# Down projection by seven products: product 2 moved ahead of product 7, and two groups of bank-emptying sums given priority on VectorE

## The chip, the cores and the metric

The kernel runs on one core of a Trainium2 chip. The metric is the time of one execution on the device in microseconds (us). Engines are named as in the profile: PE is TensorE (PEld its weight loads), DVE is VectorE, ACT is ScalarE, POOL is GpSimd, SP is SyncE, which issues most DMAs (SPq and POOLq are the queues).

## The reference

One layer of a hybrid trunk on 1024 tokens of width 1024. The change touches only the last part, the feed-forward block:

```
h2 = rms_norm(x, pre_ffn_g[l])
f = (jax.nn.silu(h2 @ w_gate[l]) * (h2 @ w_up[l])) @ w_down[l]
x = x + rms_norm(f, post_ffn_g[l])
```

The hidden width is 2816. All values are float32. The last product, with `w_down`, is called the down phase here, and the last line, a normalisation over the 1024 columns of each token and a sum, is written row by row behind it.

## The kernel before, in words

**Seven products in place of eight.** The down phase treats its two operands as 2 x 2 quadrants (two halves of 512 tokens; two halves of 512 output columns; the hidden width in 11 pairs of 128-row blocks, p = 0 to 10) and forms seven products of sums of quadrants in place of eight plain ones. Each product q is 11 steps (q, p), so there are 77 steps. The list `PQ` sets the order of the products, here 1, 5, 6, 3, 7, 2, 4. The sums of the activations were written to DRAM earlier (`fd`, `fs`) and are read back (L1106); `w_down` is read by L1112; the differences of weights for products 7 and 4 are made on VectorE by L1135.

**Exact operands by splitting.** Each operand of a step is split into a rounded part, made by ScalarE (L78, CAST), and a remainder, made by VectorE (L79). A step then has three matmuls (L1151 rounded x rounded, L1152 rounded x weight remainder, L1153 activation remainder x rounded) for each of four token strips t of 128 tokens: 12 matmuls of 512 columns.

**Blocks.** Steps are prepared in blocks, numbered 0 to 19: 18 blocks of four steps, one of one step, one of four. A block's split operands lie in a buffer `ob`, of which there are two. So the splits of block k+1 can begin when the matmuls of block k-1 are over, that is, when those of block k begin; a full block is 48 matmuls. Raw operands come through a ring of eight tiles of 256 KB, so the loads for a block's steps are issued as the splits of the block before free them. The steps of the last block run strip by strip (all four steps of t = 0, then t = 1, ...), those of all other blocks step by step.

**Banks.** Products accumulate in eight PSUM banks, one per strip: X[t] for products 1, 6, 7 and 4, which run on in the same bank, and Z[t] for 5 and 3, which run on, and for 2, which starts anew. When a product is complete, `after(q, t)` takes out strip t: products 1, 5 and 6 are copied by ScalarE (`kept`); product 3 is added to what was kept of 6 (L1191), 7 to 5 (L1196), 2 to 1 (L1201), all on VectorE; product 4 is read from the bank as it is. Products 3 and 2 give the two column halves of the first token half, 7 and 4 those of the second.

**Rows.** With both column halves of a strip at hand, the chain for its rows is: square and sum on ScalarE (L1164), gain product on GpSimd (L1167), row factor on GpSimd (L1176, L109, L111), two scalings with the sum of x on VectorE (L1182), two writes of 256 KB (L1183). The x of a strip is read from DRAM scratch (`x1d`, L1173). For the first token half this chain hangs on product 2, for the second on product 4.

**What sets the order.** The order of each engine's queue is set at build time by a scheduler that goes by program order and priority; `tc.high_priority()` moves what stands in it ahead. The splits and loads of a block stand in it. At run time each engine takes its queue strictly in that order, and so a waiting instruction holds up all behind it. The changed lines:

Of the kernel before, what the change touches and what calls it, by code (L numbers as in the profile page):

```python
# [11 lines left out]
ALU = mybir.AluOpType  # L12
# [29 lines left out]
def tile_hymba_trunk(ctx, tc, x, w_in, vecs, w_l, w2, a2, g2, w_o, w_gate, w_up, w_down,  # L42
                     gains, consts, out):
    nc = tc.nc
    te, ve, sc, gp, sy = nc.tensor, nc.vector, nc.scalar, nc.gpsimd, nc.sync
# [24 lines left out]
    def wt(name, tag, shape, dtype=F32):  # L70
        return mp.tile(shape, dtype, name=name, tag=tag, bufs=RING[tag])
# [905 lines left out]
    class Gemm:  # L977
# [55 lines left out]
        def after(self, q):  # L1033
            if q == 1:
                self.c11 = wt("c11", "bv", [128, H])
                sc.copy(self.c11, self.X)
            elif q == 2:
                ve.tensor_tensor(out=self.c11, in0=self.Y, in1=self.c11, op=ALU.add)
                self.finish(self.c11, self.c11, 0, 0)
            elif q == 6:  # L1040
                self.c12 = wt("c12", "ez", [128, H])
                sc.copy(self.c12, self.X)  # L1042
            elif q == 7:
                self.c22 = wt("c22", "am", [128, H])
                sc.copy(self.c22, self.X)
                ve.tensor_tensor(out=self.c22, in0=self.Z, in1=self.c22, op=ALU.add)
                self.finish(self.c22, self.c22, 1, 1)
            elif q == 4:
                self.finish(self.X, wt("c21", "e", [128, H]), 1, 0)
            elif q == 3:  # L1050
                ve.tensor_tensor(out=self.c12, in0=self.Z, in1=self.c12, op=ALU.add)
                self.finish(self.c12, self.c12, 0, 1)
# [22 lines left out]
    NP = NHID // 2  # L1075
# [21 lines left out]

    load_gain(1, "KB")
    XT = ["AK"] * 2 + ["Lo"] * 2 + ["Atok"] * 2
    PQ = [1, 5, 6, 3, 7, 2, 4]  # L1100
    steps = [(q, p) for q in PQ for p in range(NP)]
    tres = {}

# [34 lines left out]
    def down_block(block):  # L1138
        ob = tp.tile([128, 4, 2, 2, H], F32R, name="ob", tag="T")
        with tc.high_priority():  # L1140
            for n, (q, p) in enumerate(block):
                split(f_raw(q, p), ob[:, n, 0, 0], ob[:, n, 0, 1])
                split(d_operand(q, p), ob[:, n, 1, 0], ob[:, n, 1, 1])
        return ob

    def down_mm(q, p, ob, n, t):
        f, w = ob[:, n, 0], ob[:, n, 1]
        ts = slice(t * 128, (t + 1) * 128)
        ps = (Z if q in (5, 3, 2) else X)[t]
        st, en = q in (1, 5, 2) and p == 0, p == NP - 1  # L1150
        te.matmul(ps, lhsT=f[:, 0, ts], rhs=w[:, 0], start=st, stop=False, skip_group_check=True)  # L1151
        te.matmul(ps, lhsT=f[:, 0, ts], rhs=w[:, 1], start=False, stop=False, skip_group_check=True)  # L1152
        te.matmul(ps, lhsT=f[:, 1, ts], rhs=w[:, 0], start=False, stop=en, skip_group_check=True)  # L1153

    X, Z = [], []
# [4 lines left out]
    def square(i, dh, src):  # L1160
        if i not in ssq:
            ssq[i] = sp.tile([128, 2], F32, name="ssf", tag=f"ssf{i}", bufs=1)
        junk = wt("junk", "Vtok", [128, H])
        sc.activation(junk, src, AF.Square, accum_out=ssq[i][:, dh:dh + 1])  # L1164

    def scaled(a, dh, eng):
        eng.tensor_tensor(out=a, in0=a, in1=gain[1][:, dh * H:(dh + 1) * H], op=ALU.mult)  # L1167

    def row_scale(i):
        xts = []  # L1170
        for dh in range(2):
            xt = wt("xt", XT[(2 * i + dh) % len(XT)], [128, H])
            sy.dma_start(out=xt, in_=x1d[i * 128:(i + 1) * 128, dh * H:(dh + 1) * H])  # L1173
            xts.append(xt)
        ss = sp.tile([128, 1], F32, name="ss1", tag="ss1")
        gp.tensor_tensor(out=ss, in0=ssq[i][:, 0:1], in1=ssq[i][:, 1:2], op=ALU.add)  # L1176
        return xts, rsqrt_rows(sp, ss, D, "fo", gp)

    def row_out(i, cs, xts, rs):
        for dh in range(2):  # L1180
            a = cs[dh]
            ve.scalar_tensor_tensor(out=a, in0=a, scalar=rs, in1=xts[dh], op0=ALU.mult, op1=ALU.add)  # L1182
            sy.dma_start(out=out[i * 128:(i + 1) * 128, dh * H:(dh + 1) * H], in_=a)  # L1183

    def after(q, t):
        if q in KEPT:
            k = kept[q, t] = wt("kept", KEPT[q][t], [128, H])
            sc.copy(k, (Z if q == 5 else X)[t])
        elif q == 3:
            c = kept[6, t]  # L1190
            ve.tensor_tensor(out=c, in0=Z[t], in1=c, op=ALU.add)  # L1191
            square(t, 1, c)
            scaled(c, 1, gp)
        elif q == 7:
            c = kept[5, t]
            ve.tensor_tensor(out=c, in0=X[t], in1=c, op=ALU.add)  # L1196
            square(4 + t, 1, c)
            scaled(c, 1, gp)
        elif q == 2:
            c = kept[1, t]  # L1200
            ve.tensor_tensor(out=c, in0=Z[t], in1=c, op=ALU.add)  # L1201
            square(t, 0, c)
            scaled(c, 0, gp)
            row_out(t, (c, kept[6, t]), *row_scale(t))
        else:
            square(4 + t, 0, X[t])
            a = wt("c21", "bv", [128, H])
            ve.tensor_tensor(out=a, in0=X[t], in1=gain[1][:, 0:H], op=ALU.mult)
            row_out(4 + t, (a, kept[5, t]), *row_scale(4 + t))
# [3 lines left out]
    for bn, size in enumerate(sizes):  # L1213
        block = steps[s0:s0 + size]
        s0 += size
        ob = down_block(block)
        if bn == len(sizes) - 1:
            for t in range(4):
                for n, (q, p) in enumerate(block):
                    down_mm(q, p, ob, n, t)  # L1220
                after(q, t)
            continue
        for n, (q, p) in enumerate(block):
            if p == 0 and q == 1:
                X += [pB.tile([128, H], F32, name="pdx", tag="b") for t in range(4)]
            elif p == 0 and q == 5:
                Z += [pA.tile([128, H], F32, name="pdz", tag="a") for t in range(2)]
                Z += [pS.tile([128, H], F32, name="pdz", tag=f"c{t}") for t in range(2)]
            for t in range(4):
                down_mm(q, p, ob, n, t)  # L1230
            if p == NP - 1:
                for t in range(4):
                    after(q, t)


# [64 lines left out]
```

## Time and profile before

| | |
|---|---|
| median of three runs | 1303.29 us (1300.52 to 1306.16) |
| the profiled execution | 1306.03 us |
| its span, first to last instruction | 1304.3 us |
| TensorE busy | 1244.5 us, 95% |
| VectorE busy | 941.3 us, 72% |
| ScalarE, GpSimd busy | 540.5 us (41%), 328.5 us (25%) |
| mean granted clock of TensorE | 0.983 |

The span is the time between the first and the last instruction of the profiled execution; its own time is 1.7 us longer. A busy share is an average over all phases. The down phase is the last fifth of the span, from about 1075 us on. A granted clock of 1.00 is 2.4 GHz and 0.50 is 1.2 GHz.

### The profile page before, as it was taken

Reading aid. Unit: us, or ns where it says so; the run is one execution under the profiler, and the core shown is the slowest. Engines: PE = TensorE matmul, PEld = TensorE weight load, DVE = VectorE, ACT = ScalarE, POOL = GpSimd, SP = SyncE. Lnnn points to the kernel's source line nnn. Section 1 sums busy time; section 2 is a strip of 40 time slices with the busy share of each in tenths; the row PEclk is TensorE's granted clock in tenths of the full one; section 3 lists DMA queues with packets and bytes.
Section 4 is the critical chain, followed back from the end, with each engine's and each line's share of the span. In section 5 each row is a group of like instructions: output and inputs, shape, how many; then the busy total and the mean of one; then the engine's idle time right before and its main releaser. Section 6 shows DMA issues by size and latency. Waiting matters only on the chain.

```text
span 1304.3 us, 21097 instructions
## 1 busy us (share of the span) xinstructions
PE 1244.5 (95%) x7924; PEld 1005.8 (77%) x7924; DVE 941.3 (72%) x1784; ACT 540.5 (41%) x1029; POOL 328.5 (25%) x370
## 2 busy tenths in 40 slices
PE   6999999999999999999889999999999999999996
PEld 5878767787777778677677888888888878888884
DVE  5999797988899895563796665565665666666766
ACT  7327436445433332534353333333333353454532
POOL 2121314322232211022543234233323310000212
PEclk9999899999999999999999999999999999999999
DMA  7116332322222112652312322233323248765656
GB/s 243 33 43 207 98 130 98 105 82 87 80 94 68 42 34 74 202 170 98 137 65 98 112 82 102 100 114 113 105 81 114 90 165 276 255 195 172 210 187 210
DMA packets 76119, 162.13 MB, mean 124 GB/s; under 512 B 8880, under 2 KB 9264, under 8 KB 74608
## 3 DMA queue, kind: packets, MB, share of 16 engines
q1 hardware_dynamic: 66128, 126.96, 30.2%
q0 software_dynamic: 6432, 27.53, 5.5%
q10 hardware_dynamic: 3456, 6.29, 1.3%
q8 instruction: 62, 1.02, 0.3%
q14 instruction: 41, 0.34, 0.1%
HBM read 115.39 MB, written 45.35 MB: 123 GB/s over the span
## 4 chain that ended last, share of the span: by engine, by line
PE 45%; DVE 2%; POOL 1%; DMA 1%; issue 1%; ACT 1%; DVEq 0%; SPq 0%; ACTq 0%; POOLq 0%
PE px L1028 6%; PE px L1029 6%; PE px L1030 6%; PE pz L1028 3%; PE pz L1029 3%; PE pz L1030 3%; PE pdx L1152 2%; PE pdx L1153 2%; PE pdx L1151 2%; PE pdz L1152 2%; PE pdz L1151 2%; PE pdz L1153 2%; PE py L1030 1%; PE py L1029 1%; PE py L1028 1%
## 5 line engine op out<-in xcount | busy, mean ns | idle before, releaser
L78 ACT CAST whi<-wraw 128x512 fp32r<-128x512 f32 x111 | 68.6, 620 | 138.1 <-PE px L1029 57.9
L79 DVE TENSOR_TENSOR wlo<-wraw,whi 128x512 fp32r<-128x512 f32 x111 | 78.4, 708 | 53.8 <-ACT whi L78 53.2
L79 DVE TENSOR_TENSOR ob<-wraw,ob 128x512 fp32r<-128x512 f32 x132 | 86.2, 706 | 27.7 <-ACT ob L78 27.6
L78 ACT CAST whi<-wsum 128x512 fp32r<-128x512 f32 x88 | 54.5, 619 | 122.7 <-PE py L1029 36.1
L78 ACT CAST ob<-wraw 128x512 fp32r<-128x512 f32 x132 | 73.2, 618 | 75.1 <-PE pdx L1153 35.0
L79 DVE TENSOR_TENSOR wlo<-wsum,whi 128x512 fp32r<-128x512 f32 x88 | 68.7, 780 | 45.1 <-ACT whi L78 44.6
L250 DVE SCALAR_TENSOR_TENSOR cfa<-cfu,vec,cfa 128x512 f32<-128x512 f32 x120 | 92.3, 799 | 0.8
L103 PE MATMUL prkv<-hT,whi 128*128 128x512 f32 x192 | 82.7, 431 | 5.0 <-DVE lz L369 2.5
L580 DVE TENSOR_TENSOR tm<-TT,Mg 128x2 f32<-128x2 f32 (+30 forms) x248 | 77.7, 313 | 6.0
L993 POOL TENSOR_TENSOR wsum<-wraw 128x512 f32<-128x512 f32 x44 | 59.5, 1353 | 85.7 <-DVE wlo L79 37.7
L105 PE MATMUL prkv<-hT,wlo 128*128 128x512 f32 x192 | 78.1, 407 | 0.0
L104 PE MATMUL prkv<-hT,whi 128*128 128x512 f32 x192 | 78.0, 406 | 0.0
L1152 PE MATMUL pdx<-ob 128*128 128x512 f32 x176 | 69.3, 394 | 4.6 <-DVE ob L79 4.6
L1028 PE MATMUL px<-h2T,whi 128*128 128x512 f32 x176 | 69.8, 397 | 2.1 <-ACT c L1042 1.7
L1029 PE MATMUL px<-h2T,whi 128*128 128x512 f32 x176 | 69.5, 395 | 0.0
L1030 PE MATMUL px<-h2T,wlo 128*128 128x512 f32 x176 | 69.4, 394 | 0.0
L1151 PE MATMUL pdx<-ob 128*128 128x512 f32 x176 | 68.9, 393 | 0.0
L1153 PE MATMUL pdx<-ob 128*128 128x512 f32 x176 | 68.8, 392 | 0.0
L582 DVE TENSOR_REDUCE TT<-tm 128x1 f32<-128x2 f32 (+30 forms) x248 | 63.0, 254 | 6.0
L1167 POOL TENSOR_TENSOR kept<-kept,gain 128x512 f32<-128x512 f32 x12 | 16.7, 1410 | 169.1 <-ACT junk L1164 169.1
L1151 PE MATMUL pdz<-ob 128*128 128x512 f32 x132 | 51.3, 389 | 0.0
L1152 PE MATMUL pdz<-ob 128*128 128x512 f32 x132 | 51.3, 389 | 0.0
(360 smaller groups left out, 3458.7 us busy)
## 6 DMA issues: line engine op xcount, KB each, us to landing
wraw<-in_w_down SPq DMA_DIRECT2D x88, 256.0 KB, 4.0
wraw<-in_w_in SPq DMA_DIRECT2D x44, 256.0 KB, 2.9
wraw<-in_w_gate SPq DMA_DIRECT2D x44, 256.0 KB, 2.7
wraw<-in_w_up SPq DMA_DIRECT2D x44, 256.0 KB, 2.9
fs<-fs POOLq DMA_DIRECT2D x11, 1024.0 KB, 4.6
wraw<-fs SPq DMA_DIRECT2D x44, 256.0 KB, 3.9
fd<-c POOLq DMA_DIRECT2D x33, 256.0 KB, 2.4
wraw<-fd SPq DMA_DIRECT2D x33, 256.0 KB, 4.1
```

What stands on the lines that cost most here:

```text
L78: sc.copy(hi, raw)
L79: ve.tensor_tensor(out=lo, in0=raw, in1=hi.bitcast(F32), op=ALU.subtract)
L103: te.matmul(ps, lhsT=lhi, rhs=rhi, start=start, stop=False)
L104: te.matmul(ps, lhsT=lhi, rhs=rlo, start=False, stop=False)
L105: te.matmul(ps, lhsT=llo, rhs=rhi, start=False, stop=stop)
L250: ve.scalar_tensor_tensor(out=acc, in0=u[:, q:q + H], scalar=v1(V_CFW + i * 31 + q), in1=acc, op0=ALU.mult, op1=ALU.add)
L1028: te.matmul(ps, lhsT=hi[:, k, :], rhs=rhi, start=first and k == 0, stop=False, skip_group_check=True)
L1029: te.matmul(ps, lhsT=hi[:, k, :], rhs=rlo, start=False, stop=False, skip_group_check=True)
L1030: te.matmul(ps, lhsT=lo[:, k, :], rhs=rhi, start=False, stop=k == 3, skip_group_check=True)
L1151: te.matmul(ps, lhsT=f[:, 0, ts], rhs=w[:, 0], start=st, stop=False, skip_group_check=True)
L1152: te.matmul(ps, lhsT=f[:, 0, ts], rhs=w[:, 1], start=False, stop=False, skip_group_check=True)
L1153: te.matmul(ps, lhsT=f[:, 1, ts], rhs=w[:, 0], start=False, stop=en, skip_group_check=True)
```

## The change

Products 7 and 2 change places in `PQ`, so that product 2 comes fifth, 7 sixth and 4 last. The sums of product 3 (now L1192) and product 7 (now L1198) get high priority. The call of `after` moves from behind all four strips of a product's last step into the loop over strips. The arithmetic is the same.

```diff
-    PQ = [1, 5, 6, 3, 7, 2, 4]
+    PQ = [1, 5, 6, 3, 2, 7, 4]
...
         elif q == 3:
             c = kept[6, t]
-            ve.tensor_tensor(out=c, in0=Z[t], in1=c, op=ALU.add)
+            with tc.high_priority():
+                ve.tensor_tensor(out=c, in0=Z[t], in1=c, op=ALU.add)
...
         elif q == 7:
             c = kept[5, t]
-            ve.tensor_tensor(out=c, in0=X[t], in1=c, op=ALU.add)
+            with tc.high_priority():
+                ve.tensor_tensor(out=c, in0=X[t], in1=c, op=ALU.add)
...
             for t in range(4):
                 down_mm(q, p, ob, n, t)
-            if p == NP - 1:
-                for t in range(4):
+                if p == NP - 1:
                     after(q, t)
```

In the changed order, products that follow each other directly meet in the same banks in two places: 3 and 2 in Z (the border of blocks 10 and 11), 7 and 4 in X (inside block 16, whose first two steps are product 7's last and whose other two are product 4's first). Product 2 ends with the third step of block 13.

**VectorE's queue behind product 2.** Before, from the eighth remainder of block 17 on (L1201 is the sum of product 2, `ob` the split operands, `tres` a kept sum of weights):

```order
L79 TENSOR_TENSOR ob<-wraw,ob 128x512
L1201 TENSOR_TENSOR kept<-pdz,kept 128x512
L1135 TENSOR_TENSOR wraw<-wraw,tres 128x512
L1201 TENSOR_TENSOR kept<-pdz,kept 128x512
L1135 TENSOR_TENSOR wraw<-wraw,tres 128x512
L1182 SCALAR_TENSOR_TENSOR kept<-kept,for,xt 128x512 x2
L1135 TENSOR_TENSOR wraw<-wraw,tres 128x512
L1182 SCALAR_TENSOR_TENSOR kept<-kept,for,xt 128x512 x2
L79 TENSOR_TENSOR ob<-wraw,ob 128x512 x2
L1201 TENSOR_TENSOR kept<-pdz,kept 128x512 x2
```

Behind these rows come the other four L1182 with one L1135 among them, and then the eight remainders of block 19. After the change, from the seven first remainders of block 15 on (L1203 is the sum of product 2 now; the first two strips' sums and scalings stand in the same way ahead of these rows, behind block 14's remainders):

```order
L79 TENSOR_TENSOR ob<-wraw,ob 128x512 x7
L1135 TENSOR_TENSOR wraw<-tres,wraw 128x512
L79 TENSOR_TENSOR ob<-wraw,ob 128x512
L1203 TENSOR_TENSOR kept<-pdz,kept 128x512
L1135 TENSOR_TENSOR wraw<-tres,wraw 128x512
L1203 TENSOR_TENSOR kept<-pdz,kept 128x512
L1135 TENSOR_TENSOR wraw<-wraw,tres 128x512
L1182 SCALAR_TENSOR_TENSOR kept<-kept,for,xt 128x512 x2
L1135 TENSOR_TENSOR wraw<-wraw,tres 128x512
L1182 SCALAR_TENSOR_TENSOR kept<-kept,for,xt 128x512 x2
```

The two sets moved from the remainders of blocks 17 to 19 to those of blocks 14 to 16: the first now stands between blocks 14 and 15, the second between 15 and 16.

**VectorE's queue around the sums of product 7.** Before (L1196), between the remainders of block 14 and those of block 15:

```order
L1135 TENSOR_TENSOR wraw<-tres,wraw 128x512 x2
L79 TENSOR_TENSOR ob<-wraw,ob 128x512 x16
L1196 TENSOR_TENSOR kept<-pdx,kept 128x512 x4
L79 TENSOR_TENSOR ob<-wraw,ob 128x512 x8
L1135 TENSOR_TENSOR wraw<-wraw,tres 128x512 x2
```

After the change (L1198), from the first seven remainders of block 16, directly behind the rows shown above, to the eight of block 19:

```order
L79 TENSOR_TENSOR ob<-wraw,ob 128x512 x7
L1135 TENSOR_TENSOR wraw<-wraw,tres 128x512
L79 TENSOR_TENSOR ob<-wraw,ob 128x512
L1135 TENSOR_TENSOR wraw<-wraw,tres 128x512 x3
L79 TENSOR_TENSOR ob<-wraw,ob 128x512 x5
L1198 TENSOR_TENSOR kept<-pdx,kept 128x512 x4
L1135 TENSOR_TENSOR wraw<-wraw,tres 128x512 x2
L79 TENSOR_TENSOR ob<-wraw,ob 128x512 x3
L1135 TENSOR_TENSOR wraw<-wraw,tres 128x512
L79 TENSOR_TENSOR ob<-wraw,ob 128x512 x2
L1135 TENSOR_TENSOR wraw<-wraw,tres 128x512 x2
L79 TENSOR_TENSOR ob<-wraw,ob 128x512 x8
```

The sums moved from between two blocks' remainders into the middle of block 17's eight, behind the four weight differences of that block. No row of the first half's sums and scalings stands ahead of block 19's remainders any more.

**TensorE's queue at the first step of product 4.** Before, its first six rows (`ob_11858` are the split operands of block 16, `pdx_10462` and `pdx_10463` the banks X[0] and X[1]):

```order
L1151 MATMUL pdx_10462<-ob_11858 128x512 [waits Activation_49]
L1152 MATMUL pdx_10462<-ob_11858 128x512 [waits DVE_49]
L1153 MATMUL pdx_10462<-ob_11858 128x512
L1151 MATMUL pdx_10463<-ob_11858 128x512
L1152 MATMUL pdx_10463<-ob_11858 128x512
L1153 MATMUL pdx_10463<-ob_11858 128x512
```

After the change, the same six (`ob_11908` are the operands now):

```order
L1151 MATMUL pdx_10462<-ob_11908 128x512 [waits DVE_49,Activation_49]
L1152 MATMUL pdx_10462<-ob_11908 128x512
L1153 MATMUL pdx_10462<-ob_11908 128x512
L1151 MATMUL pdx_10463<-ob_11908 128x512 [waits DVE_49]
L1152 MATMUL pdx_10463<-ob_11908 128x512
L1153 MATMUL pdx_10463<-ob_11908 128x512
```

The first matmul into each bank has a wait for VectorE that it did not have.

## Rows read from the trace of the kernel before

**Rows 1.** The page, busy us (share of the span), instructions.
```profile
PE 1244.5 (95%) x7924; PEld 1005.8 (77%) x7924; DVE 941.3 (72%) x1784; ACT 540.5 (41%) x1029; POOL 328.5 (25%) x370
```

**Rows 2.** Busy time by stage, three stretches near the end (columns in first line).
```profile
core 0: us, PE busy (x) PEld busy (x) DVE busy (x) ACT busy (x) POOL busy (x), PEclk, DMA share, GB/s
...
1220.00:1270.00 50.00, 50.00 (x222) 41.40 (x221) 32.74 (x50) 22.38 (x46) 9.78 (x10) 1.00 0.57 188
1270.00:1280.00 10.00, 9.57 (x43) 7.59 (x41) 6.64 (x10) 4.71 (x11) 5.49 (x10) 1.00 0.64 211
1280.00:1290.00 10.00, 5.80 (x18) 4.39 (x19) 7.10 (x12) 1.45 (x4) 1.19 (x2) 0.83 0.73 230
```

**Rows 3.** Timeline of TensorE, blocks 18 and 19: start, us, instruction, [idle before].
```profile
1276.47 0.39 PE L1151 MATMUL pdx<-ob 128*128 128x512 f32 x1
...
1279.19 0.39 PE L1151 MATMUL pdx<-ob 128*128 128x512 f32 x1
1283.98 0.50 PE L1152 MATMUL pdx<-ob 128*128 128x512 f32 x1 [4.41 <-DVE ob L79]
...
1285.19 0.80 PE L1152 MATMUL pdx<-ob 128*128 128x512 f32 x1 [0.22 <-DVE ob L79]
...
1296.50 0.39 PE L1153 MATMUL pdx<-ob 128*128 128x512 f32 x1
```

**Rows 4.** Timeline of VectorE, the two sets of product 2.
```profile
1262.55 0.68 DVE L1201 TENSOR_TENSOR kept<-pdz,kept 128x512 f32<-128x512 f32 x1
...
1272.72 1.28 DVE L79 TENSOR_TENSOR ob<-wraw,ob 128x512 fp32r<-128x512 f32 x2
1273.92 1.28 DVE L1201 TENSOR_TENSOR kept<-pdz,kept 128x512 f32<-128x512 f32 x2
...
1282.64 4.90 DVE L79 TENSOR_TENSOR ob<-wraw,ob 128x512 fp32r<-128x512 f32 x8
```

**Rows 5.** Waits from 1255 to 1300: us in total, times, longest us.
```profile
DVE kept L1182 <- POOL for L111: 5.1, 6, 2.6
```

**Rows 6.** Timeline of ScalarE, casts of blocks 14 and 16.
```profile
1222.31 4.27 ACT L78 CAST ob<-wraw 128x512 fp32r<-128x512 f32 x8 [6.65 <-PE pdx L1153]
...
1244.03 4.27 ACT L78 CAST ob<-wraw 128x512 fp32r<-128x512 f32 x8 [6.61 <-PE pdz L1153]
```

**Rows 7.** Timeline of VectorE, block 14's remainders, then product 7's sums.
```profile
1222.96 4.91 DVE L79 TENSOR_TENSOR ob<-wraw,ob 128x512 fp32r<-128x512 f32 x8 [5.12 <-ACT ob L78]
1228.39 2.73 DVE L1196 TENSOR_TENSOR kept<-pdx,kept 128x512 f32<-128x512 f32 x4 [0.52 <-PE pdx L1153]
```

**Rows 8.** Timeline of VectorE, a block's remainders while product 7's loads run.
```profile
1179.40 4.30 DVE L79 TENSOR_TENSOR ob<-wraw,ob 128x512 fp32r<-128x512 f32 x7 [5.98 <-ACT ob L78]
1184.24 0.69 DVE L1135 TENSOR_TENSOR wraw<-tres,wraw 128x512 f32<-128x512 f32 x1 [0.54 <-DMA wraw<-in_w_down]
1184.85 0.68 DVE L79 TENSOR_TENSOR ob<-wraw,ob 128x512 fp32r<-128x512 f32 x1
```

**Rows 9.** Timeline of VectorE, block 16's remainders, block 17's weight differences.
```profile
1245.34 4.30 DVE L79 TENSOR_TENSOR ob<-wraw,ob 128x512 fp32r<-128x512 f32 x7
1249.56 0.68 DVE L1135 TENSOR_TENSOR wraw<-wraw,tres 128x512 f32<-128x512 f32 x1
...
1253.92 0.69 DVE L1135 TENSOR_TENSOR wraw<-wraw,tres 128x512 f32<-128x512 f32 x1 [3.08 <-DMA wraw<-in_w_down]
1255.21 0.69 DVE L1135 TENSOR_TENSOR wraw<-wraw,tres 128x512 f32<-128x512 f32 x1 [0.60 <-DMA wraw<-in_w_down]
1256.53 0.69 DVE L1135 TENSOR_TENSOR wraw<-wraw,tres 128x512 f32<-128x512 f32 x1 [0.62 <-DMA wraw<-in_w_down]
```

**Rows 10.** Busy time by stage, two stretches at the lower clock (columns as in rows 2).
```profile
1285.20:1288.20 3.00, 3.00 (x7) 2.44 (x8) 2.34 (x4) 0.00 (x0) 0.00 (x0) 0.50 0.81 178
152.00:158.40 6.40, 6.21 (x47) 5.46 (x48) 4.71 (x12) 2.73 (x7) 1.43 (x2) 0.50 0.01 3
```

**Rows 11.** Timeline of VectorE, the last scaling.
```profile
1299.99 0.74 DVE L1182 SCALAR_TENSOR_TENSOR c<-c,for,xt 128x512 f32<-128x512 f32 x1
```

## The prediction

> **What bounds the kernel now.** I read the page's busy shares first. TensorE is busy 95% of the span and VectorE 72% [rows 1], so a change in the down phase is worth only what it does to TensorE's waits and to the work behind the last matmul. The table by stage comes next: from 1220 to 1270 us TensorE has no idle time at all, and its two poor stretches are 1270 to 1280 and 1280 to 1290, the second with a granted clock of 0.83 [rows 2]. TensorE's own timeline says what happens there. Twelve matmuls of block 18 take 1279.19 - 1276.47 = 2.72 us, 0.2267 us each; a block of 48 takes 10.88. Counted back from 1276.47, blocks 17, 16, 15, 14 and 13 start at 1265.59, 1254.71, 1243.83, 1232.95 and 1222.07. In block 19 TensorE stands still for 4.41 and 0.22 us, both times for a VectorE remainder (L79), and then runs slow [rows 3]. Blocks 18 and 19 hold 60 matmuls, whose last would start at 1276.47 + 59 x 0.2267 = 1289.85; it starts at 1296.50. So **6.65 us are lost** at the end: 4.63 idle and 2.0 at the lower clock, 1.2 GHz (0.50 in the clock row [rows 10]).
>
> The cause is on VectorE's timeline. Product 2's sums come out in two sets of two strips. The first set holds the queue from 1262.55 to 1272.72 (10.17 us), the second from 1273.92 to 1282.64 (8.72 us), and only then do the remainders of block 19 start [rows 4]. Within a set VectorE waits for GpSimd's row factor [rows 5]: the two scalings (L1182) need the square on ScalarE, then the gain product and the factor on GpSimd, strip after strip.
>
> **The change part by part.** *The end.* With product 2 fifth, nothing of it stands ahead of the remainders of block 19; the order shows the eight remainders right behind two L1135. They can start only when block 17's operand buffer is free. At such a start the first remainder follows 0.89 us behind the block's first matmul (1222.96 against 1222.07), and eight take 4.91 [rows 7]. Block 18 covers 2.72 us; block 19 wants a pair of remainders every 0.68 us, and VectorE makes one every 1.23. The fourth pair is ready at 0.89 + 4.91 = 5.80 after block 18's start, and wanted at 2.72 + 3 x 0.68 + 0.23 = 4.99, so 0.8 us stay (0.9 with signals). The gain at the end is 6.65 - 0.9 = **5.75 us**. What follows the last matmul (1296.50 to 1304.3) keeps its order and its length: the last scaling is at 1299.99 there [rows 11], and the output goes behind it.
>
> *Product 3 into 2.* Product 2's first matmul into each Z bank now waits for that strip's sum. The four sums stand behind block 11's remainders, which are done some 5.8 us into block 10, ahead of the last step of product 3. Four such sums took 2.73 us, and started 0.2 us behind their bank's last matmul [rows 7]. A strip is needed again 2.04 us after its own last matmul, and a sum takes 0.7. I take nothing; if the cover went, it would be 0.7.
>
> *Product 2's two sets, now in blocks 13 to 16.* I follow VectorE's queue by the order after the change. Block 14's first seven remainders start at 1222.96. In the same place before, seven remainders from 1179.40, a weight difference that waits for its load, and the eighth ended the turn 6.05 us later (1184.85 + 0.60) [rows 8]. So the first set starts at 1222.96 + 6.05 = 1229.0; product 2's last step is then through (in before the sums of the product in that place started at 1228.39). The set is as long as before, 8.72 to 10.17; I take the middle, 9.4, since a weight difference still stands between the two sums but its load is less late. It ends at 1238.4. Block 15's remainders start there, 4.6 us later than they could, and still 5.4 us ahead of block 15: no stall. They take 6.05 to 1244.5, and the second set 9.4 to **1253.9**. Only then do block 16's remainders start. Block 16 is due at 1254.71 and its second matmul needs the second remainder, 1.3 us in: a stall of about 0.3 us.
>
> *Product 7 into 4.* This is the term that decides. Product 7 ends in the second step of block 16, and product 4's first matmul, in its third step, waits for L1198. L1198 stands in VectorE's queue behind the rest of block 16's remainders, four L1135 and five remainders of block 17. The fourth L1135 waits for the eighth of eight loads. In before, with the same loads in the same place, the remainders of block 16 started at 1245.34 and these L1135 at 1249.56, 1253.92, 1255.21 and 1256.53: the last at +11.19 [rows 9]. So, from 1253.9: the last L1135 ends at +11.8, five remainders at +14.9, the first sum at +15.6, which is **1269.5**. TensorE would be there, without stalls, at 1254.71 + 5.44 = 1260.15. The wait is **9.35 us**, in which the 0.3 us of block 16 is contained. It follows the start of block 16's remainders one for one: with both sets at 8.72 it is 8.0, with both at 10.17 it is 10.9, and had they started at 1244.6 it would be none (their buffer is free with block 15's start at 1243.83; the casts of the same block began at 1244.03 in before [rows 6]). The other three sums follow 0.6 us apart, faster than TensorE's 0.68 per strip.
>
> The Trainium skill (Perfetto Trace Analysis, Optimizing Tensor Performance, Matmuls) says that independent groups of matmuls should rotate through different PSUM banks, so that the eviction of one lies beside the next group's matmuls; the new order gives that up in two places. By that rule and the row of the four sums alone the price would be nothing, since a sum of 0.7 us lies inside the 2.04 us of the other strips. The 9.35 us come from what is queued ahead of the sums, of which the rule says nothing.
>
> *Clock.* After 4.63 us of waits TensorE lost 2.0 us at the lower clock. After 9.35 I take 1.9. The lower end is 1.5 (half of the 3.0 us row), the upper 3.2, half of 6.4 us at clock 0.50, the longest such stretch I found [rows 10].
>
> *Behind it.* Block 17 starts near 1277, 11.5 us late, and VectorE's remaining L1135 and remainders for blocks 17 and 18 are through by about 1287, ahead of block 18 (1288): hidden. More output writes and reads of x1d fall between weight loads, but no more of them in all.
>
> **The sum.** Lost after the change: 9.35 + 1.9 + 0.9 = 12.15 us; before: 6.65. The end comes 5.5 us later: span 1304.3 to 1309.8, the profiled execution 1306.03 to 1311.5. The median of the runs shown, 1303.29, lies 2.7 below that execution, so I forecast **1309 us**, 0.43% slower. From no change a measurement here can tell about 0.5%, 6.5 us.
>
> **The rivals.**
> *It goes as meant, and is faster.* One mechanism: the factor chain on GpSimd is hidden in the middle, so that block 16's remainders start near 1244.6 and L1198 is there in time. Then 5.75 us are gained: 1297.5. For it: VectorE is idle about a third of 1220 to 1270 (32.74 busy of 50 [rows 2]). Against it: the queue is in order, both sets of before took over 8.7 us, and the second starts behind the first. It decides at a wait of some 3.8 us (5.75 less 1.9 for the clock), a start before 1248.4, for which both sets together would have to be 5.5 us shorter than my 18.8.
>
> *The stall is there, but moderate.* If loads for block 17 land earlier, or the sets overlap better, 4 to 6 us of wait and 1.9 of clock cancel the gain: 1303 to 1305.5. Against it: the loads of that place are measured.
>
> *It is longer.* Eight row writes and several reads of x1d (256 KB each) now lie between the weight loads of blocks 15 to 17, where the engines of DMA are 57% busy [rows 2]. If they delay the loads that L1135 waits for by 1 to 2 us in both places, and the lower clock holds for 6.4 us, the wait is 11 to 13 and the clock 3.2: 1311.5 to 1314. A wait for loads of up to 3 us inside this queue speaks for it [rows 9].
>
> *It does nothing.* The order of all engines does move, so this can only be an exact cancelling; it is in the moderate case.
>
> **How the numbers follow.** Chances: forecast (1307 to 1311) 0.6, longer 0.17, moderate 0.13, faster 0.1. The limit for slower, 1309.8, cuts the forecast's case: two fifths of it lie above (0.24), and nearly all of the longer case (0.17), hence slower 0.41. The faster case gives 0.44%, just inside the limit, so less than half of it counts: 0.04. The rest, 0.55, is within 0.5%. Range: 1302.5 to 1314 leaves out the faster case and the tails.
>
> **What would show it.** The waits of TensorE should list pdx L1151 waiting for a DVE sum of L1198, 9 us, near 1260, and a half-clock stretch behind it; block 19's wait for L79 should fall from 4.41 to under 1; the two sets should take 8.7 to 10.2 us each and end near 1238 and 1254. I am wrong if block 16's remainders start before 1248, if the fourth L1135 behind them comes much earlier than +11.2, or if what follows the last matmul changes its length.

## The result, and the profile after

The changed kernel takes 1311.8 us (median of 8 runs, 1308.26 to 1315.74), the kernel before, beside it, 1303.43: a ratio of 1.0076 (95% interval 1.0060 to 1.0092), 8 to 12 us slower. The forecast was 1309, and its range, 1302.5 to 1314, holds the time. The profiled execution took 1315.74 us with a span of 1314.0. One execution of the experiments below, of the kernel with the scalings behind block 17, took 3628 us and is in no ratio.

On the page (answers to [rows 1]) hardly anything moves:

```profile
PE 1247.6 (95%) x7924; PEld 1007.9 (77%) x7924; DVE 946.2 (72%) x1784; ACT 540.9 (41%) x1029; POOL 329.9 (25%) x370
```

The waits of TensorE, from 1060 us to the end, in the changed kernel (us in total, times, longest):

```profile
PE pdx L1151 <- DVE kept L1198: 6.3, 1, 6.3
PE pdx L1152 <- DVE ob L79: 3.2, 1, 3.2
```

The 4.41 us in block 19 [rows 3] are gone. In their place stand two waits in block 16: its second matmul waits for a remainder, and its third step, product 4's first, for a sum of product 7. TensorE's timeline there (start, us, instruction, [idle before]):

```profile
1257.04 0.39 PE L1151 MATMUL pdx<-ob 128*128 128x512 f32 x1
1260.62 0.50 PE L1152 MATMUL pdx<-ob 128*128 128x512 f32 x1 [3.19 <-DVE ob L79]
...
1261.49 0.63 PE L1152 MATMUL pdx<-ob 128*128 128x512 f32 x1
...
1267.34 0.39 PE L1153 MATMUL pdx<-ob 128*128 128x512 f32 x1
1274.01 0.76 PE L1151 MATMUL pdx<-ob 128*128 128x512 f32 x1 [6.28 <-DVE kept L1198]
1274.57 0.63 PE L1152 MATMUL pdx<-ob 128*128 128x512 f32 x1
...
1281.62 0.39 PE L1151 MATMUL pdx<-ob 128*128 128x512 f32 x1
...
1306.16 0.39 PE L1153 MATMUL pdx<-ob 128*128 128x512 f32 x1
```

Block 16 starts at 1257.04 and the next at 1281.62: 24.58 us for a block that takes 10.88, so 13.7 lost, 9.47 of them idle. The rest is nearly all the lower clock, here in busy time by stage (columns in the first line; the clock is the column PEclk):

```profile
core 0: us, PE busy (x) PEld busy (x) DVE busy (x) ACT busy (x) POOL busy (x), PEclk, DMA share, GB/s
1254.00:1280.00 26.00, 16.52 (x56) 12.65 (x55) 21.52 (x30) 10.42 (x22) 9.04 (x9) 0.80 0.68 234
...
1260.50:1263.00 2.50, 2.38 (x7) 1.89 (x8) 2.50 (x6) 0.29 (x1) 0.00 (x0) 0.67 0.71 214
1263.00:1267.00 4.00, 4.00 (x15) 3.21 (x15) 2.02 (x4) 1.58 (x3) 0.00 (x0) 0.78 0.87 264
...
1273.50:1278.00 4.50, 3.99 (x10) 3.15 (x11) 4.24 (x6) 2.61 (x8) 3.30 (x3) 0.50 0.73 252
```

There are two stretches at the lower of the two levels, one behind each wait. VectorE's timeline shows what was late (answers to [rows 4] and [rows 9]):

```profile
1226.40 0.69 DVE L1135 TENSOR_TENSOR wraw<-tres,wraw 128x512 f32<-128x512 f32 x1 [0.93 <-DMA wraw<-in_w_down]
1227.01 4.30 DVE L79 TENSOR_TENSOR ob<-wraw,ob 128x512 fp32r<-128x512 f32 x7
...
1233.11 0.68 DVE L1203 TENSOR_TENSOR kept<-pdz,kept 128x512 f32<-128x512 f32 x1
...
1242.69 4.30 DVE L79 TENSOR_TENSOR ob<-wraw,ob 128x512 fp32r<-128x512 f32 x7
1248.89 0.69 DVE L1135 TENSOR_TENSOR wraw<-tres,wraw 128x512 f32<-128x512 f32 x1 [1.90 <-DMA wraw<-in_w_down]
...
1250.10 0.68 DVE L1203 TENSOR_TENSOR kept<-pdz,kept 128x512 f32<-128x512 f32 x1
...
1254.47 2.44 DVE L1182 SCALAR_TENSOR_TENSOR kept<-kept,for,xt 128x512 f32<-128x512 f32 x2 [1.00 <-POOL for L111]
...
1259.28 4.29 DVE L79 TENSOR_TENSOR ob<-wraw,ob 128x512 fp32r<-128x512 f32 x7
...
1269.56 0.69 DVE L1135 TENSOR_TENSOR wraw<-wraw,tres 128x512 f32<-128x512 f32 x1 [0.75 <-DMA wraw<-in_w_down]
1270.17 3.09 DVE L79 TENSOR_TENSOR ob<-wraw,ob 128x512 fp32r<-128x512 f32 x5
1273.18 2.48 DVE L1198 TENSOR_TENSOR kept<-pdx,kept 128x512 f32<-128x512 f32 x4
...
1309.66 0.74 DVE L1182 SCALAR_TENSOR_TENSOR c<-c,for,xt 128x512 f32<-128x512 f32 x1
```

The two sets of product 2 run from 1233.11 to 1242.69 and from 1250.10 to 1259.28. Block 16's remainders start behind the second, 2.2 us after TensorE reached that block, and the sums of product 7 behind four weight differences and five remainders of block 17. From the last scaling (1309.66) to the end it is 4.34 us, as in [rows 11].

**A measure for all that follows.** The down phase does not start at the same time in every profiled execution: its first matmul lies at 1071.37 us before and at 1073.95 after, and in the other traces of this study anywhere from 1064.08 to 1073.95. So traces are compared by the time from that matmul to the end of the span: 1304.3 - 1071.37 = 232.9 us before, 1314.0 - 1073.95 = 240.1 after, 7.1 more.

### The profile page after: what moved, and what is told of

The parts are those of the page before. It is cut to its first block, busy times and chain, and to the rows that moved or that the text cites. A ratio compares the mean times of both kernels' runs of the same rounds, so it can differ in the third digit from the quotient of the medians.

```text
span 1314.0 us, 21092 instructions
## 1 busy us (share of the span) xinstructions
PE 1247.6 (95%) x7924; PEld 1007.9 (77%) x7924; DVE 946.2 (72%) x1784; ACT 540.9 (41%) x1029; POOL 329.9 (25%) x370
## 4 chain that ended last, share of the span: by engine, by line
PE 42%; DVE 3%; DMA 3%; POOL 1%; issue 1%; ACT 0%; DVEq 0%; SPq 0%; ACTq 0%; POOLq 0%
PE px L1028 6%; PE px L1029 6%; PE px L1030 6%; PE pz L1028 3%; PE pz L1029 3%; PE pz L1030 3%; PE pdx L1151 2%; PE pdx L1152 2%; PE pdx L1153 2%; DVE ob L79 2%; DMA wraw<-in_w_down 2%; PE pdz L1151 2%; PE pdz L1153 2%; PE pdz L1152 1%; PE py L1030 1%; PE py L1029 1%
## 5 line engine op out<-in xcount | busy, mean ns | idle before, releaser
L79 DVE TENSOR_TENSOR ob<-wraw,ob 128x512 fp32r<-128x512 f32 x132 | 88.9, 727 | 30.0 <-ACT ob L78 29.9
L103 PE MATMUL prkv<-hT,whi 128*128 128x512 f32 x192 | 82.5, 430 | 5.1 <-DVE lz L369 2.6
L993 POOL TENSOR_TENSOR wsum<-wraw 128x512 f32<-128x512 f32 x44 | 59.8, 1359 | 86.4 <-DVE wlo L79 47.7
L1151 PE MATMUL pdx<-ob 128*128 128x512 f32 x176 | 70.0, 399 | 6.3 <-DVE kept L1198 6.3
L1152 PE MATMUL pdx<-ob 128*128 128x512 f32 x176 | 70.2, 399 | 3.2 <-DVE ob L79 3.2
L1153 PE MATMUL pdx<-ob 128*128 128x512 f32 x176 | 69.7, 397 | 0.0
L1167 POOL TENSOR_TENSOR kept<-kept,gain 128x512 f32<-128x512 f32 x12 | 18.2, 1532 | 164.6 <-ACT junk L1164 164.6
```

The lines of the kernel that those rows point to most:

```text
L79: ve.tensor_tensor(out=lo, in0=raw, in1=hi.bitcast(F32), op=ALU.subtract)
L103: te.matmul(ps, lhsT=lhi, rhs=rhi, start=start, stop=False)
```

## The experiments

Each ratio is against the kernel before, run on the same chip beside it (its medians there were 1300.5 to 1302.0 us). "Phase" is the measure above from one profiled execution, with its difference to 232.9. The waits are TensorE's, in blocks 14 to 19. Line numbers shift by a few between the kernels; a `kept` that a matmul into `pdx` waits for is always a sum of product 7, an `ob` a split operand.

| kernel | ratio (95% interval) | phase, us | waits, us |
|---|---|---|---|
| the changed kernel again | 1.0061 (1.0041 to 1.0082) | 238.2 (+5.3) | 1.1 + 8.3 |
| order without priority | 1.0078 (1.0047 to 1.0108) | 243.3 (+10.4) | 2.6 + 9.4 |
| sums of product 7 first | 1.0043 (1.0025 to 1.0060) | 236.7 (+3.7) | 8 waits, 7.2 |
| row writes last | 1.0066 (1.0045 to 1.0087) | 237.6 (+4.6) | 1.0 + 7.6 |
| scalings behind blocks 15 and 16 | 1.0031 (1.0016 to 1.0047) | 233.5 (+0.5) | 3.8 |
| scalings behind block 17 | 1.0004 (0.9983 to 1.0025) | 231.0 (-1.9) | 3.2 |
| the same, ring of 12 | 1.0067 (1.0049 to 1.0086) | 237.1 (+4.1) | 1.6 |
| changed kernel, ring of 12 | 1.0123 (1.0102 to 1.0144) | 247.5 (+14.6) | 7.9 |
| old order, scalings behind 18 and 19 | 0.9996 (0.9981 to 1.0011) | 229.0 (-3.9) | none |
| old order, scalings behind 18 | 0.9961 (0.9943 to 0.9978) | 227.7 (-5.3) | 0.8 |
| the same, ring of 12 | 1.0055 (1.0036 to 1.0075) | 236.9 (+4.0) | none |
| the same, ring of 12 from block 12 on | 0.9960 (0.9943 to 0.9977) | 226.9 (-6.0) | none |

**The theories.** Mine was the queue: TensorE waits because of what stands ahead of a VectorE instruction in VectorE's queue. The rivals: the banks (products 7 and 4 meeting in the same four banks cost the time by themselves), and the loads (row writes and reads of x among the weight loads, or the ring of raw operands, make the loads late).

**The changed kernel again.**

> The changed kernel itself, once more, beside the others on this chip. If its trace is the rule, the down phase loses 6.5 to 7.5 us more than in the kernel before, in two waits of 3 and 6 us with the lower clock behind each; the ratio should be 1.006 to 1.009 again. If the start of the down phase differs by up to 10 us between executions for reasons ahead of it, it will differ here too.

Its waits, from 1060 us on:

```profile
PE pdx L1151 <- DVE kept L1198: 8.3, 1, 8.3
PE pdx L1152 <- DVE ob L79: 1.1, 1, 1.1
```

They sum to 9.4 again (9.47 in the first trace), divided otherwise. Behind the shorter one the granted clock stayed at 1.00, so there was one stretch of the lower clock and not two, and the phase is 1.8 us shorter.

**Order without priority.** The edit takes the priority from the sums of products 3 and 7.

```diff
-            with tc.high_priority():
-                ve.tensor_tensor(out=c, in0=X[t], in1=c, op=ALU.add)
+            ve.tensor_tensor(out=c, in0=X[t], in1=c, op=ALU.add)
```

> The changed kernel without the priority of the sums: only the order of the products and the place of the call are changed. The sums of product 7 then stand behind all eight of block 17's remainders and behind more weight differences on VectorE. Queue theory: the first matmul of product 4 waits longer, 9 to 12 us in place of 6.3, 3 to 6 us slower than the changed kernel. Bank theory: the same time as the changed kernel, since the banks meet in the same way.

```profile
PE pdx L1151 <- DVE kept L1196: 9.4, 1, 9.4
PE pdx L1152 <- DVE ob L79: 2.6, 1, 2.6
```

The banks meet exactly as before, and the waits grow from 9.4 to 12.0 us, because the sums now stand behind all eight remainders of block 17. The wait follows the queue. Against the changed kernel on the same chip that is 2.85 us by the medians (1312.28 and 1309.43); the intervals of the two ratios overlap, so by the times alone the help of the priority is not shown, and the 2.6 us of waits are what speaks for it.

**Sums of product 7 first.** Block 17's remainders and weight differences are kept behind the four sums: while `pin` is set, the scheduler may not move them ahead (the lines of this kernel are shifted by 6).

```diff
+        pin[0] = bn == 17
         ob = down_block(block)
+        pin[0] = False
```

> The changed kernel with one edit: block 17's remainders and weight differences are kept behind the four sums of product 7 on VectorE, so these sums follow block 16's remainders directly. Product 2's two sets stay where the change put them. Queue theory (TensorE waits because of what stands ahead of a VectorE instruction in its in-order queue): the wait of product 4's first matmul for a sum of product 7, 6.3 us in the changed kernel, falls to about 0.7 us; the wait of 3.2 us for block 16's remainders stays, with about 2 us of half clock behind it; 1303 us, 8 to 9 us under the changed kernel. Bank theory (products 7 and 4 meeting in the same four banks costs the time by itself): the wait stays near 6 us and the time near 1311.8. Load theory (row writes and reads of x among the weight loads make the loads late): the sums come earlier, but block 17's operands then come as late as before, and the wait moves to the start of block 17: 1309 to 1312.

The wait for a sum is gone; the waits in its place (TensorE, 1200 to 1310, then ScalarE, 1250 to 1285):

```profile
PE pdx L1158 <- DVE ob L85: 4.2, 5, 2.6
PE pdx L1157 <- ACT ob L84: 2.9, 3, 1.4
...
ACT ob L84 <- DMA wraw<-fd: 9.3, 4, 4.6
ACT ob L84 <- DVE wraw L1141: 8.8, 3, 4.2
```

Of the 8 to 9 us that the queue theory expected, 2 to 4 came (1.0043 against 1.0061 and 1.0076 for the changed kernel). The longest wait, 2.6 us, is still the one for block 16's second remainder, which the edit does not touch. Nearly all the rest is for the operands of block 17. Their casts wait for loads and for weight differences that stand behind the late work, and the loads were issued only when block 16's late remainders gave their tiles back. So the sums were the first thing to be late, not the only one: the sets push back a whole chain of remainders, loads and weight differences. The load theory had expected this shift, though with less gain.

**Row writes last.** The eight writes of the first half are issued behind block 19's loads. A scaling of the second set moves with it, behind block 16's remainders.

> The changed kernel with one edit: the eight row writes of the first token half are issued behind block 19's weight loads on SyncE's queue, so none lies among the weight loads of blocks 15 to 17 (the last scaling of the second set moves behind block 16's remainders with it). Load theory: the loads come earlier, the weight differences wait less, and 2 to 5 us are won back: 1307 to 1310. Queue theory: the sets are as long as before (9 to 9.6 us), the two waits of 3.2 and 6.3 us stay within 1 us each (the one scaling that moved makes 0.7 us less of the first), 1310 to 1312.

The waits sum to 8.5 in place of 9.4, and the ratio is that of the changed kernel. VectorE still waits 9.8 us for loads between 1225 and 1285, against 9.7 with the writes in between. The writes are not the cause. The reads of x, which the load theory named beside them, stayed among the weight loads; no run moves them away.

**Scalings out of the sets.** The scalings of product 2 (L1182 in the changed kernel) are collected and emitted later, first two strips each behind the remainders of blocks 15 and 16, then all behind block 17's (there with a ring of eight x tiles).

```diff
-            row_out(t, (c, kept[6, t]), *row_scale(t))
+            late.append((t, (c, kept[6, t]), *row_scale(t)))
...
         ob = down_block(block)
+        if bn == 17:
+            for x in late:
+                row_out(*x, pin=True)
```

> The changed kernel with one edit: product 2's four sums stay behind block 14's remainders, its eight scalings (and their row writes) stand two strips each behind block 15's and behind block 16's remainders, so that VectorE does not stand still for GpSimd's row factor. The order of the products, the priority of the sums and all transfers stay. Queue theory: no wait at block 16, 0 to 1 us at the first matmul of product 4, 0.3 at the end: 1297 to 1298 us, faster than both kernels. Bank theory: the wait for the sum of product 7 stays near 6 us, the time near 1311. Load theory: the writes and reads still lie among the weight loads, the fourth weight difference of block 17 comes as late as before, and at least half of the 6.3 us stays: 1303 to 1307.

> The changed kernel, new order of products and priority kept, with all eight scalings of product 2 behind block 17's remainders, so that none stands ahead of the sums of product 7 any more, and a ring of eight x tiles. With two strips each behind the remainders of blocks 15 and 16 a wait of 3.8 us for a sum of product 7 was left, with 5.6 us of scalings ahead of it in the queue. Queue theory: that wait goes to 0 to 0.5 us, the end loses 0.3 us: 5 to 6 us faster than before, as much as the old order gets from the same deferral. Bank theory: 3 to 4 us of wait stay whatever stands ahead, about no change. Load theory: the fourth weight difference of block 17 is still late by its loads, 1 to 3 us of wait stay, 2 to 4 us faster.

Neither went as the queue theory had it. The first left 3.8 us and lost 0.3% to the kernel before; the second, with no scaling ahead of the sums at all, still left 3.2 and came out even. The waits of the second (TensorE, 1200 to 1310; VectorE, 1210 to 1285):

```profile
PE pdx L1151 <- DVE kept L1202: 3.2, 1, 3.2
...
DVE wraw L1135 <- DMA wraw<-in_w_down: 15.0, 15, 2.9
```

With the sets' waits out of the way, VectorE still waits 15.0 us for the loads of weight differences. That is no more than elsewhere. Over all 22 differences (1150 to 1300 us) it waits, in the kernel before and in the changed one:

```profile
DVE wraw L1135 <- DMA wraw<-in_w_down: 18.2, 15, 3.7
...
DVE wraw L1135 <- DMA wraw<-in_w_down: 17.4, 15, 3.2
```

What differs is where they fall. In the new order products 7 and 4, which both need these differences, follow each other, and the 22 stand in one run of 68 us (1213 to 1281 us here). In the old one product 2, which needs none, stands between them: eleven from 1184 to 1212, eleven from 1243 to 1280. A second thing may hold a part of the 3.2 us: GpSimd's row factors now run beside block 15's remainders, the first seven of which take 6.53 us in place of 4.30 (last section). No run separates the two.

**A larger ring of raw operands.** Four more tiles, so that a block's loads need not wait for the last remainders of the block before.

```diff
+    RAWS += ["Mg", "QM", "yz", "t2r"]
```

> New order of products, priority kept, all eight scalings of product 2 behind block 17's remainders, as in the run before that left a wait of 3.2 us for a sum of product 7; the one difference is the ring of raw operands, 12 tiles in the down phase in place of 8, so that the loads for a block need not wait for the last remainders of the block before. Load theory (what is left of the wait is VectorE standing still for loads: 10.5 us of such waits between 1212 and 1260 there): these waits fall to under 3 us in all, the wait for a sum of product 7 to under 1, 4 to 6 us faster than the kernel before. Queue theory in its narrow form (only what VectorE has to do counts): the 3.2 us stay. Bank theory: they stay too.

> The changed kernel with one difference, the ring of raw operands, 12 tiles in the down phase in place of 8 (the sets of product 2 stand where they stood, but with no or one weight difference less ahead of the next remainders). Load theory alone (the waits for loads are the whole cost): both waits of TensorE go, 5 to 6 us faster than the kernel before. Queue and loads together: the two sets still take 7 to 9 us each for the row factor of GpSimd, block 16's remainders start some 2 us earlier and the sums of product 7 some 4 us earlier: 2 to 5 us of wait and one fall of the clock stay, 1 us faster to 2 us slower than before. Queue theory in its narrow form: as the changed kernel, 7 to 9 us slower than before.

```profile
PE pdx L1153 <- DVE kept L1204: 1.6, 1, 1.6
...
DVE wraw L1137 <- DMA wraw<-in_w_down: 11.5, 14, 1.6
```

These are the waits of the first (same stretches); in the second the wait for a sum of product 7 is 7.9. Both kernels are slower, at another place: with the larger ring a cast in the first blocks of the phase waits 9.0 us for its operand (10.2 in the second), and TensorE behind it 6.2 (8.1). In blocks 14 to 19 alone the four runs, one trace each, divide the cost: 9.4 us of waits, 7.9 with the ring, 3.2 without the scalings, 1.6 with both. Taking the scalings out is worth 6.2, the ring behind it 1.6, and 1.6 is left.

**The old order with the scalings later.** Here the order of products, and with it the banks, is that of the kernel before; only the scalings move, first behind the remainders of blocks 18 and 19, then all behind block 18's, and the ring of x tiles has eight.

> The kernel before, with its old order of products and no priority for sums, and one edit: product 2's four sums stay ahead of block 19's remainders, its eight scalings stand two strips each behind block 18's and behind block 19's remainders; the ring for the x of the rows has eight tiles in place of six, since these reads come later. Queue theory: the 4.6 us of waits in block 19 fall to 0.8, the lower clock behind them goes too, 5 to 6 us less than before: 1297 to 1299 us, 1 to 3 more if the late row writes delay the last rows. The new order would then not be needed for the gain that was to be had. Bank theory: says nothing against it (no banks are shared by neighbours here), the same 1297 to 1299. If the wait in block 19 has another cause than the scalings (the loads, or the remainders' own rate), it stays and the time is about 1303.

> The kernel before, old order of products, no priority, with all eight scalings of product 2 behind block 18's remainders (VectorE stood idle for 3.9 us there with four of them) and a ring of eight x tiles; the row writes then go out ahead of the reads of x for the last rows instead of between them. In the kernel with the last four scalings behind block 19's remainders the wait in block 19 was gone (6.5 us less lost by TensorE) but the work behind the last matmul was 10.4 us long in place of 7.8, the last scalings waiting 2.1 us for x. Queue theory: no wait in block 19, the end 7.5 to 9 us long again: 5 to 6.5 us faster than before. If the eight scalings in one piece hold block 19's remainders up, 1 to 2 us of the wait come back, 3 to 5 us faster. If what that run lost beyond its own trace (its median is 3 us above what the trace of one execution gives) hangs on the deferral itself, about no change.

In the first, TensorE does not wait at all in the down phase, as expected, and the gain is lost again behind the last matmul. VectorE's timeline there:

```profile
1285.29 0.75 DVE L1184 SCALAR_TENSOR_TENSOR kept<-kept,for,xt 128x512 f32<-128x512 f32 x1 [0.64 <-DMA xt<-x1d]
1288.16 0.75 DVE L1184 SCALAR_TENSOR_TENSOR c<-c,for,xt 128x512 f32<-128x512 f32 x1 [2.12 <-DMA xt<-x1d]
```

The last scalings wait for x, because its reads stand in SyncE's queue behind row writes that wait for the late scalings and for those of the last rows. From the last matmul to the end it is 10.4 us in place of 7.8. In the second, SyncE's timeline shows the writes ahead of the reads, all issued before the last rows:

```profile
1270.83 6.62 SPq L1187 DMA_DIRECT2D out<-kept  x8
1277.50 3.79 SPq L1173 DMA_DIRECT2D xt<-x1d  x8
```

There 0.8 us of waits are left, the end is 7.0 us long, and the kernel is 0.39% faster than the one before (0.22 to 0.57%): 5.1 us by the ratio, 5.3 by the trace.

**The old order with the ring of 12**, from the start of the phase and from block 12 on:

> The old order of products with all eight scalings behind block 18's remainders, which was 5 us faster than the kernel before, and the ring of 12 raw operands. The 0.8 us of waits left in block 19 there are for the rate of its remainders or for the last weight difference, which waits for its load; the larger ring lets that load start earlier: 5 to 7 us faster than before, at best 1 to 1.5 us under the same with a ring of eight. If the loads at the border between the phases now collide with other transfers, no gain over it.

> The old order of products, all eight scalings behind block 18's remainders, and the ring of 12 raw operands from block 12 on only, since a ring of 12 from the start cost 9 to 11 us in the first blocks of the down phase (a cast there waited 9.0 us for its operand) and won 1.8 us at the end. If the cost at the border came from the ring there, it is gone, no wait is left in block 19, and TensorE loses at most 0.5 us there in place of 6.7: 6 to 7.5 us faster than the kernel before, the best of all versions. If the cost comes from the larger ring itself wherever it begins (more loads in flight beside the others), 2 to 9 us are lost where it begins.

The first pays at the border as above (a cast waits 10.1 us there), the second does not, so it is the ring there that costs. The waits in block 19 are gone in both. The gain of the second over the ring of eight, 0.8 us in the trace, is too small for the ratios (0.9960 and 0.9961). These two old-order versions are the only ones here that beat both kernels.

## Why the prediction was right, point by point

*The end.* Right, a little undersized: blocks 18 and 19 lose 0.3 us where 0.9 was forecast. What follows the last matmul kept its length, 7.8 us.

*Product 3 into 2.* Right: TensorE does not wait at that border.

*The two sets.* Their lengths, 9.58 and 9.18 us against 9.4, are right, and so is the queue between them. They end later than forecast, at 1242.69 and 1259.28; taking off the 2.58 us by which the whole phase started later, that is 1240.1 and 1256.7, where 1238.4 and 1253.9 stood. The step that failed is what lies between them: block 14's remainders were late behind a weight difference that waited for its load (1.5 us), and block 15's turn took 7.41 us in place of 6.05, since a difference waited 1.90 us for its load. So the stall at block 16 was 3.2 us, not 0.3.

*Product 7 into 4.* The wait was forecast as 9.35 us with the stall of block 16 contained; the idle time is 9.47 in one trace and 9.38 in the other. In the first trace that agreement is luck in part: block 16's remainders came 2.8 us later than forecast, the sum 1.0 us earlier behind them (+13.9 us in place of +14.9), and the stall at block 16 made TensorE itself late. Counted as the forecast did, from where product 4's first matmul would have started without stalls (1257.04 + 5.44), it started 11.5 us late, of which some 2 lie behind the first wait, most of them at the lower clock. In the second trace the steps fit too: counted so it was 9.8 us late. The mechanism holds: without priority, with the same banks, the waits are 12.0; without the scalings, 3.2.

*The rule on banks.* By the Trainium skill (Perfetto Trace Analysis, Optimizing Tensor Performance, Matmuls) independent groups of matmuls should rotate through different banks. The prediction counted two places where the new order gives that up. Only one is such a pair: product 2 starts anew in Z behind product 3, and there TensorE did not wait. Product 4 adds on to what products 1, 6 and 7 left in X, so in this scheme it has to meet product 7's banks. The runs can bound what that meeting costs by itself: with the scalings away and the ring larger the wait is 1.6 us, so at most that. The other 7.8 of the 9.4 are the queue and the loads.

*Clock.* Mis-sized in the profiled execution: 4.2 us were lost beside the idle time (13.7 - 9.47), nearly all at the lower clock, where 1.9 was taken and 3.2 was the upper end. I had one wait and one fall; there were two of each. With one fall, in the second trace, it is 2.3 (11.66 us lost in block 16, 9.38 of them idle), inside the forecast's bounds.

*The sum.* Forecast +5.5 us; by the two traces +7.1 and +5.3; by the ratios +9.9 (1.0076) and +7.9 (1.0061). So the working accounts for the 5 to 7 us that the traces place in the down phase; the 2 to 3 us that the ratios add are not explained by it.

*The rivals.* "It goes as meant" fell with the sets, which took 18.8 us together, as forecast. Of the longer case, delayed loads were there, but not by the row writes: with the writes moved out the loads wait as long.

*What I got wrong afterwards.* In the experiments I treated the queue as if only the instructions in it counted. Freeing the sums alone gave 2 to 4 us of 8 to 9; freeing the queue of all scalings gave back the loss, but not the 5 to 6 us that I expected beyond it. What most likely holds the rest is a loop: remainders free the tiles, the loads follow, the differences wait for the loads, and the next remainders stand behind the differences. That two products in a row which need differences leave this loop no slack is argued, from the queue and from where the differences fall. The waits for loads do not show it by their sum (15.0 us here, 18.2 in the kernel before), and the ring bears it out only in part (3.2 to 1.6 us).

*Still open.* For most kernels the ratio says 2 to 5 us more than the phase of their trace (the changed kernel +9.9 against +7.1, the scalings behind blocks 15 and 16 +4.0 against +0.5); for the order without priority and for the old order with the scalings behind block 18 the two agree. There is one profiled execution of the kernel before, and whether it lost more than others of its kind was not tried. Why the larger ring makes the first cast wait at the border was not followed up.

## What to carry to other kernels

Before moving a producer away from the end of a queue, ask whether the stall comes from its place or from what it waits for: here the eight scalings waited for a row factor, and taking them out of the way in the old order gave 5 us once their writes went out ahead of the reads of x, while moving the whole product cost 8 to 10. Work that waits for another engine belongs behind the instructions that feed the critical engine, at a point where the queue has idle time, and its DMAs ahead of those that the end needs. And when one late instruction is freed, look at what its neighbours were late for as well: if buffers come free by the same queue, the loads are late too.

## What the runs showed of the hardware

- **Short waits and the clock.** In the late blocks, a wait of 3.2 us or more was followed by a stretch at the lower level each time (granted clock 0.50 to 0.67 there, 1.7 to 2.5 us lost behind each by the spacing of the matmuls). Waits of 1.0 to 1.6 us were not. Of two waits of 2.6 us one was followed by a granted clock of 0.57, the other by 1.00.
- **VectorE beside GpSimd.** The same operation on VectorE took longer while GpSimd computed: block 15's seven remainders in the kernel with the scalings behind block 17 took 6.53 us, block 14's 4.30. In busy time by stage of those two stretches:

```profile
1224.57:1228.87 4.30, 4.30 (x21) 3.56 (x20) 4.30 (x8) 2.61 (x6) 0.00 (x0) 1.00 0.52 169
1237.56:1244.09 6.53, 6.53 (x30) 5.40 (x30) 6.53 (x8) 3.61 (x7) 6.27 (x8) 1.00 0.53 168
```

  GpSimd is busy 0.00 and 6.27 us in them. The Trainium skill (SBUF — State Buffer, SBUF: two separate sides) says that the two engines share a pair of ports, which one of them holds for a whole instruction, also when the VectorE instruction merely has two inputs in SBUF and the GpSimd instruction reads SBUF. A remainder has two such inputs; the longer remainders agree, the wait itself is not in the trace. The forecast had no such term: in the changed kernel three remainders behind the sums of product 7 took 4.08 us, at 1278.14, though TensorE did not wait for them.
- **The start of the phase.** Traces of kernels that are alike up to there reach the down phase up to 10 us apart. Most of it arises between 375 and 630 us: the earliest and the latest are 2.7 us apart at the last L103 of `prkv` (374.6 and 377.3) and 10.5 at the first sum of L993 on GpSimd (628.5 and 639.0). From 550 to 600 the granted clock was 1.00 in the earliest (old order, scalings behind 18 and 19), 0.93 in the latest (the changed kernel).
